# RWKV-7 chunk recurrence: two dependent products per chunk, or one prebuilt map

## The chip, the core and the metric

One Trainium2 chip, one of its cores, one launch. The metric is the device time of that core in microseconds (us), the median of repeated executions. The profile's own execution is told apart from them below.

## What is computed

A two-layer decoder step for 512 prompt positions and 8 x 4 sample positions, width 1024, 16 heads of 64. Layer A is RWKV-7 time mixing, layer B attention in three dilated windows. The part that matters here is layer A's scan over the prompt, for each head a 64 x 64 state:

```python
def wkv_step(state, inp):
    r, w, k, v, kk, b = inp
    sa = jnp.einsum('bhij,bhj->bhi', state, kk)
    state = state * w[:, :, None, :] - sa[..., None] * b[:, :, None, :] + v[..., None] * k[:, :, None, :]
    return state, jnp.einsum('bhij,bhj->bhi', state, r)

wkv, ys = lax.scan(wkv_step, wkv_prev.astype(f32), seq)
```

The outputs `ys` go through a group norm and a gate to the layer's output; the last state is an output too.

## The kernel before

All activations lie with features on the partitions: eight tiles of 128 features (two heads each), 544 positions (512 prompt, 32 sample). `dense` (L152) does the projections: each fp32 weight tile is split into a high and a low part, and three matmuls of 256 or 288 columns per 128 features of input give one output tile. Layer A needs 40 such projections, layer B 88.

The scan is done in 8 chunks of 64 positions. With the decays folded into the operands, a chunk is linear: its corrections solve a triangular system of 64 x 64, whose inverse T is computed once (`tinv`, `tmerge`), and then the new state and the outputs follow from the old state and the chunk's values. Head pairs p = 0 to 7 are processed one after the other and partly side by side. For each p:

- `pre_a`, `pre_b`, `gram` build the scaled operands: RH (receptance), BK (per chunk, 64 columns of b and 64 of k), AK (masked products with k, and the keys kk transposed). `tinv` runs on DVE for two head pairs at once, 62 dependent operations; `tmerge` joins its blocks on PE.
- `prechain(p)`, L607: T is multiplied into AK, 32 matmuls of 64 x 64 x 64, copied by ACT. The result WW is the left operand that turns [state; values] into the corrections u.
- `feed(p, i)`, for the chunks 2i and 2i+1, needs two PSUM buffers of tag "u" (there are two in all; `tmerge`, `prechain` and `gn` use them too). It forms Q = BK^T RH for both heads (L624, names qvp and qbp after their buffers) and masks it on DVE (L631), transposes the values (L628) and copies them on DVE to the lower half of `mv` (tiles of 128 rows: 64 of state, 64 of values), multiplies BK by the chunk's decay on POOL (L641), transposes it (L643), and copies it back on ACT.
- `step(p, i)` runs the two chunks one after the other. Per chunk and head: u = WW^T mv (L656); ACT copies u beside the values into `uv` (line of the helper `mv_`, L104; POOL has copied the values there); state product BK^T uv (L661); DVE adds the decayed old state and writes the next chunk's `mv` (L671); outputs from the state (L675) and from `uv` with Q (L678) into one sum. DVE copies the pair's outputs to Y.

Two chunks of one head pair depend on each other through L656, the ACT copy, L661 and L671. Different head pairs, feeds, and the projections of z and v are independent of that chain.

The order of the program is a list of tokens (`PLAN`: K, r, v, z are projections, a, b, e the operands, T, M, P the inverse, F a feed, C a step, G, I the group norm). The framework's scheduler turns it into one order for each engine when the kernel is built: it takes the tokens' order as priority, its own estimate of durations, and the free buffers. So each engine's order is fixed before the run, and an engine waits at its next instruction whatever stands behind. `NQ` = 4 fed chunk pairs may be ready at a time. `ENG` says which engine does a copy (s is ACT, v DVE, g POOL).

## Time and profile before

| what | us |
|---|---|
| median of 3 runs (1506.02 to 1510.37) | 1506.65 |
| the profiled execution | 1502.82 |
| its span, first to last instruction | 1501.0 |
| PE busy (matmuls; their pipelined ends are modelled) | 1373.4 |
| DVE busy | 989.5 |
| ACT busy | 654.1 |
| POOL busy | 531.5 |
| mean granted PE clock, 1 is full speed | 0.925 |

The profile gives each engine's instructions by line of the kernel. An fp32 matmul appears as two instructions. In a group's row stand the line, the engine, the operation, the tile that it writes and those that it reads, the shapes and the count; then the busy time and the mean of one in ns, and the idle time of that engine just ahead, with the engine and line that ended it. A timeline's row begins with the start and the duration in us. PE is the matmul, PEld the load of its weights.

### The profile page before, as it was taken

How to read it: one execution, taken by the hardware profiler on the slowest of the kernel's cores; microseconds unless marked ns; L12 is line 12 of the kernel's file. 1: busy time of each engine (PE TensorE's matmuls, PEld its weight loads, DVE VectorE, ACT ScalarE, POOL GpSimd, SP SyncE). 2: the span in 40 equal slices, each digit the busy share in tenths (PEclk: the TensorE clock that was granted, in tenths of full speed). 3: DMA queues.
4: the chain of work that ended last, by engine and by line, in shares of the span. 5: the costliest groups of instructions: out<-in, count | busy, mean ns of one | idle time of the engine just before them, and what ended most of it. 6: DMA issues, size and time to landing. Idle time of an engine off the chain costs nothing.

```text
span 1501.0 us, 32052 instructions
## 1 busy us (share of the span) xinstructions
PE 1373.4 (91%) x12144; PEld 1161.3 (77%) x12144; DVE 989.5 (66%) x2612; ACT 654.1 (44%) x1808; POOL 531.5 (35%) x763
## 2 busy tenths in 40 slices
PE   2999879998988998999889899999999999999986
PEld 2777868676767666989777779989799888998776
DVE  7428594747677546798996869756568554685434
ACT  5448353333342355444543435545355543644321
POOL 6124365434545221796867686000000000000121
PEclk9999978765879698999999999999999999999988
DMA  4123636224243113456344583445734356344632
GB/s 145 46 80 132 201 97 157 62 56 122 66 123 72 38 43 116 150 165 202 90 136 147 171 269 120 145 142 164 256 111 151 129 194 232 103 152 136 227 116 102
DMA packets 140587, 201.26 MB, mean 134 GB/s; under 512 B 76864, under 2 KB 80640, under 8 KB 140432
## 3 DMA queue, kind: packets, MB, share of 16 engines
q1 hardware_dynamic: 121456, 137.48, 29.9%
q10 hardware_dynamic: 16416, 54.41, 10.8%
q0 software_dynamic: 2560, 7.31, 1.4%
q8 instruction: 96, 1.57, 0.4%
q14 instruction: 59, 0.48, 0.1%
HBM read 150.90 MB, written 34.87 MB: 124 GB/s over the span
## 4 chain that ended last, share of the span: by engine, by line
PE 42%; DVE 8%; DMA 3%; ACT 1%; issue 1%; SPq 1%; ACTq 0%; DVEq 0%
PE dps L152 29%; DVE wlo L139 4%; PE sps L1014 3%; PE ptp L1075 2%; PE spo L1170 2%; PE ops L1091 1%; DMA swp<-nat 1%; PE ops L1087 1%; PE sc L1126 1%; SPq L945 1%; PE sc L1137 1%; PE sc L1132 1%; PE vtp L975 1%; DVE swp L947 1%; DMA vc<-in_vc 1%
## 5 line engine op out<-in xcount | busy, mean ns | idle before, releaser
L152 PE MATMUL dps<-hn,whi 128*128 128x256 f32 (+1 forms) x2560 | 509.3, 294 | 8.2 <-DVE vt L964 2.4
L152 PEld LDWEIGHTS dps<-hn,whi 128*128 128x128 f32 x2560 | 405.3, 189 | 31.0 <-issue 19.0
L152 PE MATMUL dps<-hn,wlo 128*128 128x288 f32 (+1 forms) x1280 | 373.6, 292 | 5.0 <-DVE wlo L139 4.6
L138 ACT ACTIVATE whi<-wst,prm 128x128 fp32r<-128x128 f32 x640 | 202.1, 391 | 223.2 <-PE dps L152 173.4
L139 DVE SCALAR_TENSOR_TENSOR wlo<-wst,prm,whi 128x128 fp32r<-128x128 f32 x640 | 252.7, 450 | 35.2 <-ACT whi L138 34.6
L152 PE MATMUL dps<-x,whi 128*128 128x256 f32 (+1 forms) x1024 | 229.7, 317 | 27.4 <-ACT x L166 11.0
L152 PEld LDWEIGHTS dps<-hn,wlo 128*128 128x128 f32 x1280 | 242.8, 190 | 12.7 <-DVE wlo L139 7.6
L152 PEld LDWEIGHTS dps<-x,whi 128*128 128x128 f32 x1024 | 178.1, 207 | 52.1 <-issue 15.9
L134 POOL TENSOR_TENSOR wlo<-wst,whi 128x1024 fp32r<-128x1024 f32 x48 | 118.5, 2469 | 191.9 <-ACT whi L133 179.3
L152 PE MATMUL dps<-x,wlo 128*128 128x288 f32 (+1 forms) x512 | 158.2, 310 | 0.0
L152 PEld LDWEIGHTS dps<-x,wlo 128*128 128x128 f32 x512 | 106.4, 208 | 2.6 <-issue 1.8
L1100 POOL COPY qd<-Q 64x32 f32<-64x32 f32 x48 | 12.7, 265 | 266.4 <-DVE Q L950 143.2
L1298 POOL TENSOR_TENSOR sS<-sS,sT 128x256 f32<-128x256 f32 x128 | 102.6, 802 | 8.3 <-DMA sS<-in_stN 0.2
L152 PE MATMUL dps<-g,whi 128*128 128x288 f32 (+1 forms) x512 | 102.2, 296 | 2.9 <-DVE ho L869 1.4
L133 ACT CAST whi<-wst 128x1024 fp32r<-128x1024 f32 x48 | 50.3, 1047 | 93.8 <-PE dps L152 61.3
L152 PEld LDWEIGHTS dps<-g,whi 128*128 128x128 f32 x512 | 82.1, 191 | 6.4 <-DVE g L167 2.9
L946 DVE TENSOR_TENSOR nat<-nat,cosn 128x544 f32<-128x544 f32 x48 | 36.5, 760 | 66.4 <-DMA swp<-nat 65.5
L152 PE MATMUL dps<-g,wlo 128*128 128x256 f32 (+1 forms) x256 | 74.1, 290 | 0.0
L1029 ACT ACTIVATE s<-s,nm 128x256 f32<-128x256 f32 (+1 forms) x128 | 61.7, 484 | 20.1 <-DVE nm L1026 20.0
L1107 POOL COPY pk<-vt 128x32 f32<-128x32 f32 x24 | 5.4, 225 | 161.1 <-DVE vt L964 108.6
L1014 PE MATMUL sps<-K,Q 64*128 64x128 f32 (+1 forms) x384 | 55.1, 321 | 6.4 <-DVE st L1020 4.0
L307 DVE SCALAR_TENSOR_TENSOR mix<-xn,prm,mix 128x512 f32<-128x512 f32 x48 | 42.4, 884 | 26.0 <-ACT mix L305 25.9
(315 smaller groups left out, 2433.6 us busy)
## 6 DMA issues: line engine op xcount, KB each, us to landing
wst<-in_wb SPq DMA_DIRECT2D x88, 512.0 KB
kc<-in_kc ACTq DMA_DIRECT2D x48, 512.0 KB
vc<-in_vc ACTq DMA_DIRECT2D x48, 512.0 KB
wst<-in_wa SPq DMA_DIRECT2D x40, 512.0 KB
swp<-nat SPq DMA_DIRECT2D x192, 68.0 KB
out_kT<-K SPq DMA_DIRECT2D x24, 272.0 KB
out_vT<-vt SPq DMA_DIRECT2D x24, 272.0 KB
xt<-in_xT SPq DMA_DIRECT2D x8, 272.0 KB
```

The lines of the kernel that those rows point to most:

```text
L133: nc.scalar.copy(hi, st)
L134: nc.gpsimd.tensor_tensor(lo, st, hi.bitcast(F32), op=ALU.subtract)
L138: nc.scalar.mul(hi[:, kt], st[:, kt], g)
L139: nc.vector.scalar_tensor_tensor(lo[:, kt], st[:, kt], g, hi[:, kt].bitcast(F32), op0=ALU.mult, op1=ALU.subtract)
L152: nc.tensor.matmul(ps[:, :n], lhsT=a[:, kt, :], rhs=x[:, c0:c0 + n], start=(kt == 0 and i == 0), stop=(kt == KT - 1 and i == 2))
L307: nc.vector.scalar_tensor_tensor(m[:, 0:NP_], xn[kt][:, 0:NP_], pv(s, kt), m[:, 0:NP_], op0=ALU.mult, op1=ALU.add)
L946: nc.vector.tensor_tensor(nat, nat, cosn, op=ALU.mult)
L1014: nc.tensor.matmul(ps[h][:, j, o], lhsT=Q[g][r, q], rhs=K[g][r, ks], start=True, stop=True)
L1029: nc.scalar.activation(s[:, b, lo:], s[:, b, lo:], AF.Exp, bias=nm[:, b:b + 1], accum_out=stats[:, b, h, 1:2])
L1075: nc.tensor.transpose(ps[:, b], st["s", l, h][:, b, half * P:(half + 1) * P], self.ident)
L1170: nc.tensor.matmul(po[32 * j:32 * j + 32, 0:256], lhsT=pT[:, i, 32 * j:32 * j + 32], rhs=vc[:, j], start=(i == 0), stop=False, skip_group_ ...
L1298: nc.gpsimd.tensor_tensor(s, s, t, op=ALU.add)
```

## The change

The chunk's map is built in the feed, ahead of the step. `prechain` makes the transposed WT (16 matmuls of 64 rows, 64 outputs and 128 columns in place of 32 of 64 columns, L608). `feed` writes the masked Q (L631) and the transposed BK (now three ACT copies, since each head's parts go to different places) into one tile `yz`, multiplies it by WT in PSUM (new, L650: 64 rows, 128 outputs, 128 columns, one per chunk and head, into the same two PSUM buffers), and adds what belongs to the values (DVE, L655) and to RH (DVE, L656 of the changed file); two ACT copies ("zz") bring over the state's map. So `yz` holds, for 128 rows of [state; values], 64 columns that give the outputs and 64 that give the next state. `step` is then per chunk and head one product for the state (L666), the same DVE update (L675), and one product for the outputs (L679). `uv` and its copies are gone. In `ENG`, the values' copies `mv` and the outputs' copy `ye` move from DVE to ACT. `PLAN`, the buffers and the rest stay.

```diff
-           w="ss", mv="vv", uv="gg", bt="s", kt="v", pr="s", ak="s", yc="s", ye="v", bo="gg", w1="ssss", tt="s")
+           w="ss", mv="ss", bt="s", kt="v", pr="s", ak="s", yc="s", ye="s", bo="gg", w1="ssss", tt="s")
...
             def prechain(p):
...
-                    for h in range(2):
-                        o = 128 * c2 + 64 * h
-                        for m in (0, 64):
-                            nc.tensor.matmul(ps[e][m:m + 64, o:o + 64], lhsT=ak[q, c2, h, m:m + 64],
-                                             rhs=t[q, 2 * c2 + h, :], start=True, stop=True)
+                    for h, r in enumerate(RH2):
+                        o = P * c2
+                        nc.tensor.matmul(ps[e][r, o:o + P], lhsT=t[q, 2 * c2 + h, :], rhs=ak[q, c2, h, :],
+                                         start=True, stop=True)
...
             def feed(p, i):
...
-                qq = QQ[p, i] = sp.tile([P, 2, 2, 64], F32, name="Q", tag="Q", bufs=NQ)
+                x = YZ[p, i] = sp.tile([P, 2, 2, P], F32, name="yz", tag="Q", bufs=NQ)
                 for h in range(2):
-                    nc.vector.tensor_tensor(qq[:, h], pq[h][:, 0:128].rearrange("p (e x) -> p e x", e=2),
+                    nc.vector.tensor_tensor(x[:, :, h, 0:64], pq[h][:, 0:128].rearrange("p (e x) -> p e x", e=2),
                                             msk[:, None, 1, :].to_broadcast([P, 2, 64]), op=ALU.mult)
...
-                self.mv_("bt", b2.rearrange("p c x -> p (c x)"), pq[1][:, 256:512])
+                b = pq[1][:, 256:512].rearrange("p (e h x) -> p e h x", e=2, h=2)
+                self.mv_("bt", x[:, :, 0, 64:128], b[:, :, 0, :])
+                self.mv_("bt", x[RA, :, 1, 64:128], b[RB, :, 1, :])
+                self.mv_("bt", x[RB, :, 1, 64:128], b[RA, :, 1, :])
+                for e in range(2):
+                    for h, r in enumerate(RH2):
+                        nc.tensor.matmul(pq[h][:, P * e:P * e + P], lhsT=w[r, e, i, :], rhs=x[r, e, h, :],
+                                         start=True, stop=True)
+                for h, r in enumerate(RH2):
+                    o = RH2[1 - h]
+                    v = pq[h][:, 0:256].rearrange("p (e x) -> p e x", e=2)
+                    nc.vector.tensor_tensor(x[o, :, h, :], v[o], x[o, :, h, :], op=ALU.add)
+                    nc.vector.tensor_tensor(x[r, :, h, 0:64], v[r, :, 0:64], rh[r, 2 * i:2 * i + 2, :], op=ALU.add)
+                    self.mv_("zz", x[r, :, h, 64:128], v[r, :, 64:128], h)
...
             def step(p, c2):
...
-                        nc.tensor.matmul(ps[r, o:o + 64], lhsT=WW[p][:, e, c2, h, :], rhs=mv[:, e, h, :],
+                        nc.tensor.matmul(ps[r, o:o + 64], lhsT=x[:, e, h, 64:128], rhs=mv[:, e, h, :],
                                          start=(e == 0), stop=True, skip_group_check=True)
-                    for h, r in ((0, RA), (1, RB)):
-                        self.mv_("ue", uv[RA, e, h, :], ps[r, o:o + 64], h)
-                    for h, r in ((0, RA), (1, RB)):
-                        nc.tensor.matmul(ps[r, o + 64:o + 128], lhsT=BK[p][:, c, 64 * h:64 * h + 64],
-                                         rhs=uv[:, e, h, :], start=False, stop=True,
-                                         skip_group_check=True)
...
-                    for h, r in ((0, RA), (1, RB)):
-                        nc.tensor.matmul(ps[r, y:y + 64], lhsT=mv[r, e, h, :], rhs=RH[p][r, c, :],
-                                         start=False, stop=False, skip_group_check=True)
-                    for h, r in ((0, RA), (1, RB)):
-                        nc.tensor.matmul(ps[r, y:y + 64], lhsT=uv[:, e, h, :], rhs=qq[:, h, e, :],
+                    for h, r in enumerate(RH2):
+                        nc.tensor.matmul(ps[r, y:y + 64], lhsT=mv[:, e, h, :], rhs=x[:, e, h, 0:64],
                                          start=False, stop=True, skip_group_check=True)
```

The built order moves with it on every engine. PE of before, at the third feed of head pair 5 (buffers qvp_5420, qbp_5421) and the steps beside it:

```order
L624 MATMUL qvp_5420<-rT_3111,bk_3235 64x64 x4
L628 MATMUL qvp_5420<-ident_58,vT_3349 64x128 x2
L643 MATMUL qbp_5370<-ident_58,bk_3235 128x128 x2
L675 MATMUL cps_5394<-rT_3111,mv_5354 64x64 x2
L678 MATMUL cps_5394<-Q_5351,uv_5391 64x64 x2
L656 MATMUL cps_5394<-mv_5354,ak_3241 64x64 x2
L747 MATMUL ysp_6041<-ident_58,yt_6039 128x32
L624 MATMUL qbp_5421<-rT_3111,bk_3235 64x64 x4
L661 MATMUL cps_5394<-uv_5391,bk_3235 64x64 x2
L656 MATMUL cps_5445<-mv_5384,ak_3241 64x64
L747 MATMUL ysp_6046<-ident_58,yt_6044 128x32
L675 MATMUL cps_5394<-rT_3111,mv_5354 64x64 x2
```

PE of the changed kernel at the same feed (buffers qvp_5278, qbp_5279; L650 is the new product, its first two rows here are the feed before):

```order
L650 MATMUL qvp_5230<-yz_5242,ak_3200 128x128 x2
L650 MATMUL qbp_5231<-yz_5242,ak_3200 128x128 x2
L624 MATMUL qvp_5278<-rT_3070,bk_3194 64x64 x4
L628 MATMUL qvp_5278<-ident_58,vT_3308 64x128 x2
L666 MATMUL cps_5312<-mv_5245,yz_5242 64x64
L624 MATMUL qbp_5279<-rT_3070,bk_3194 64x64 x4
L666 MATMUL cps_5312<-mv_5245,yz_5242 64x64
L643 MATMUL qbp_5279<-ident_58,bk_3194 128x128 x2
L679 MATMUL cps_5312<-yz_5242,mv_5245 64x64 x2
L666 MATMUL cps_5312<-mv_5245,yz_5242 64x64 x2
L650 MATMUL qvp_5278<-yz_5290,ak_3200 128x128 x2
L650 MATMUL qbp_5279<-yz_5290,ak_3200 128x128 x2
```

Before, the transposes L643 of a feed stand well behind its products L624, and the next feed's products ahead of them. Now one step matmul stands between the two, two step groups between L643 and L650, and one (L679) between L650 and the next feed.

ACT of the changed kernel for the same two feeds (Y is the outputs' copy, mv the values', yz the map's):

```order
L104 COPY mv_5245<-qvp_5230 64x2x64 x2
L104 COPY Y_4552<-cps_5264 128x128
L104 COPY yz_5242<-qbp_5231 128x2x64
L104 COPY yz_5242<-qbp_5231 64x2x64 x2
L104 COPY yz_5242<-qvp_5230 64x2x64
L104 COPY yz_5242<-qbp_5231 64x2x64
L104 COPY mv_5293<-qvp_5278 64x2x64 x2
```

and of before, where the copies of two head pairs' corrections stand between those of the feeds:

```order
L104 COPY uv_5391<-cps_5394 64x64 x2
L748 COPY YS_349<-ysp_6026 128x32
L104 COPY uv_5310<-cps_5313 64x64 x2
L104 COPY bk_3235<-qbp_5340 128x256
L748 COPY YS_349<-ysp_6031 128x32
L748 COPY YS_349<-ysp_6036 128x32
L104 COPY bk_3235<-qbp_5370 128x256
L104 COPY uv_5391<-cps_5394 64x64 x2
```

Five copies of a feed now follow one another on ACT, with the feed's values ahead of them. Between the stretch's last projection and the end of the recurrence, PE's order holds 5 feeds and 8 steps before, and 8 feeds and 11 steps now.

More of the change, by code (lines that the diff above doesn't have):

```diff
@@ L590, in tmerge @@
                     self.mv_("tt", t[q, :, 32:64], ps[q, 0:256].rearrange("p (c t) -> p c t", c=8))
-            TT, WW, Y = ([None] * 8 for _ in range(3))
-            QQ, MV = {}, {}
+            TT, WT, Y = ([None] * 8 for _ in range(3))
+            YZ, MV = {}, {}
+            RA, RB = slice(0, 64), slice(64, 128)
+            RH2 = (RA, RB)
             def prechain(p):
-                ak, bk, rh, t = AK[p], BK[p], RH[p], TT[p]
+                ak, t = AK[p], TT[p]
                 w = ak.rearrange("p c h x -> p (c h x)")
-                WW[p] = w.rearrange("p (e c h x) -> p e c h x", e=2, c=4, h=2)
+                WT[p] = w.rearrange("p (e c x) -> p e c x", e=2, c=4)
                 ps = [U8("wwp") for _ in range(2)]
@@ L611, in prechain @@
                 Y[p] = np_.tile([P, 560], F32, name="Y", tag="N")[:, 0:NT]
-            RA, RB = slice(0, 64), slice(64, 128)
             def feed(p, i):
-                bk, rh = BK[p], RH[p]
+                bk, rh, w = BK[p], RH[p], WT[p]
                 pq = [U8("qvp"), U8("qbp")]
@@ L620, in feed @@
                     c = 2 * i + e
-                    for h in range(2):
-                        r = slice(64 * h, 64 * h + 64)
+                    for h, r in enumerate(RH2):
                         for m in (0, 64):
-                            nc.tensor.matmul(pq[h][m:m + 64, 64 * e:64 * e + 64], lhsT=bk[r, c, m:m + 64],
+                            o = m if h == 0 else 64 - m
+                            nc.tensor.matmul(pq[h][o:o + 64, 64 * e:64 * e + 64], lhsT=bk[r, c, m:m + 64],
                                              rhs=rh[r, c, :], start=True, stop=True)
@@ L646, in step @@
+                for h, r in enumerate(RH2):
[4 more added lines that the diff above has]
+                    self.mv_("zz", x[r, :, h, 64:128], v[r, :, 64:128], h)
             def step(p, c2):
-                uv = sp.tile([P, 2, 2, 64], F32, name="uv", tag="uv", bufs=2)
@@ L649, in step @@
[L649 to L651 removed]
+                mv, x = MV[p, c2], YZ[p, c2]
                 ps = C8("cps")
                 for e in range(2):
[L654 to L656 removed]
+                    c, o = 2 * c2 + e, 64 * e
+                    for h, r in enumerate(RH2):
+                        nc.tensor.matmul(ps[r, o:o + 64], lhsT=x[:, e, h, 64:128], rhs=mv[:, e, h, :],
```

18 lines of the change are left out of this document (7 added, 11 removed).

## The prediction, made before the result was known

> **What bounds the kernel now.** I read the page first, for the busy shares, the granted clock and the chain that ended last.
>
> ```profile
> PE 1373.4 (91%) x12144; PEld 1161.3 (77%) x12144; DVE 989.5 (66%) x2612; ACT 654.1 (44%) x1808; POOL 531.5 (35%) x763
> ...
> PEclk9999978765879698999999999999999999999988
> ...
> PE 42%; DVE 8%; DMA 3%; ACT 1%; issue 1%; SPq 1%; ACTq 0%; DVEq 0%
> ```
>
> PE is busy nine tenths of the span, and what the chain names is mostly PE. The clock digits show one bad place: slices 6 to 14. Then I asked for the windows of the stretch in which the recurrence runs and of what follows.
>
> ```profile
> 255.00:575.00 320.00, 290.21 (x3501) 215.92 (x3501) 203.21 (x605) 126.00 (x349) 128.19 (x216) 0.76 0.28 75
> 575.00:1501.00 926.00, 875.66 (x7162) 775.96 (x7160) 632.82 (x1692) 400.23 (x1206) 290.77 (x410) 0.98 0.48 158
> ```
>
> The columns are the stretch, its length, then busy time of PE, PEld, DVE, ACT and POOL, the clock, DMA share and GB/s. The recurrence takes 320 us. PE is idle for 30 of them, and its mean clock is 0.76 against 0.98 afterwards. If the clock is either 1.0 or 0.5, as the short windows below suggest, then 48% of the stretch, 154 us, is at half. Everything after 575 us is projection work that the change does not touch, so a microsecond of PE time gained or lost in the stretch is one of the span.
>
> ```profile
> 430.00:450.00 20.00, 15.56 (x194) 11.14 (x194) 18.36 (x60) 6.46 (x19) 6.34 (x10) 0.50 0.11 35
> ...
> 500.00:522.00 22.00, 20.57 (x173) 13.99 (x173) 7.84 (x29) 5.77 (x26) 3.89 (x10) 0.53 0.09 30
> 522.00:527.00 5.00, 5.00 (x37) 4.23 (x37) 4.15 (x9) 3.78 (x5) 0.85 (x3) 0.66 0.03 7
> 535.00:565.00 30.00, 27.63 (x356) 15.54 (x356) 15.39 (x52) 17.08 (x44) 8.30 (x16) 1.00 0.21 66
> ```
>
> These show three regimes. At 430 DVE is the bound (the triangular inverse), and PE idles. At 500 PE runs the small recurrence matmuls nearly without a gap, yet at half clock; the projection that begins at 522 brings the clock back. At 535 the same small matmuls run at full clock. So PE is the bound for most of the stretch, and the next question is how much of its idle time is the chain of chunks. The waits of PE between 255 and 575 us (total, times, longest):
>
> ```profile
> PE cps L675 <- DVE mv L671: 8.4, 8, 2.3
> PE atp L524 <- DVE ak L517: 4.7, 1, 4.7
> PE cps L656 <- DVE mv L104: 3.3, 2, 3.1
> ...
> PE cps L661 <- ACT uv L104: 2.1, 4, 0.7
> PE cps L656 <- DVE mv L671: 1.4, 2, 1.0
> ```
>
> Only 8.4 + 2.1 + 1.4 = 11.9 us of PE's idle time is charged to the chain that the change shortens. The chain is long, but the order fills it with other heads' work.
>
> **PE's own work.** A pair of chunks (one feed and one step; there are 32) now has 8 groups of matmuls in the step, each of 4 instructions of 64 columns. After the change it has 4 in the step, and two new groups in the feed (after's L650) of 4 instructions each, 64 rows by 128 columns. The prechain's matmuls (L607) become half as many of twice the width: nothing. For the prices I take starts of consecutive groups in the timeline:
>
> ```profile
> 265.58 1.16 PE L411 MATMUL lps<-hid,lb 64*128 64x256 f32 x2
> 266.67 0.48 PE L675 MATMUL cps<-rT,mv 64*64 64x64 f32 x4
> ...
> 500.23 0.45 PE L624 MATMUL qbp<-rT,bk 64*64 64x64 f32 x8
> 500.61 0.34 PE L656 MATMUL cps<-mv,ak 128*64 128x64 f32 x4
> ...
> 500.84 0.61 POOL L641 TENSOR_TENSOR bk<-bk,plp 128x256 f32<-128x256 f32 x1 [0.49 <-PE qbp L624]
> ...
> 508.68 0.48 PE L675 MATMUL cps<-rT,mv 64*64 64x64 f32 x4
> 509.09 0.48 PE L678 MATMUL cps<-Q,uv 128*64 128x64 f32 x4
> ...
> 509.96 0.69 PE L624 MATMUL qbp<-rT,bk 64*64 64x64 f32 x8
> 510.58 0.48 PE L661 MATMUL cps<-uv,bk 128*64 128x64 f32 x4
> ...
> 526.56 0.33 PE L675 MATMUL cps<-rT,mv 64*64 64x64 f32 x4
> 526.82 0.34 PE L678 MATMUL cps<-Q,uv 128*64 128x64 f32 x4
> ...
> 540.77 0.44 PE L643 MATMUL qbp<-ident,bk 128*128 128x128 f32 x2
> 541.13 0.34 PE L656 MATMUL cps<-mv,ak 128*64 128x64 f32 x4
> 541.64 0.27 PE L624 MATMUL qbp<-rT,bk 64*64 64x64 f32 x2 [0.17 <-DVE mv L104]
> ...
> 541.87 0.28 PE L624 MATMUL qvp<-rT,bk 64*64 64x64 f32 x4
> 542.09 0.41 PE L628 MATMUL qvp<-ident,vT 128*64 128x128 f32 x2
> ```
>
> A step group costs 0.26 us at full clock (526.56 to 526.82) and 0.41 at half (508.68 to 509.09), so the four that go are worth 1.04 or 1.64 us a pair. No row shows the new matmul. Its nearest rows are two groups of 8 of 64 rows and 64 columns, the same number of columns in all: 2 x 0.38 = 0.76 us at full clock (500.23), 2 x 0.62 = 1.24 at half (509.96). The other is the only one with 64 rows and all 128 outputs: 2 instructions of 256 columns in 1.09 us at half (265.58 to 266.67), so 2.18 for the 1024 columns needed, and by the ratio 0.41/0.26 1.38 at full. I take the middle of the two, 1.07 and 1.71, since the new operation has the rows of the first and the outputs of the second. That is +0.03 or +0.07 us a pair: **+2 us** for 32. Ends: the second row throughout gives +0.34 and +0.54, +14 us; the interleaved row (16 instructions from 541.64 to 542.09, 0.45 us, and 0.71 at half) gives -0.59 and -0.93, -24 us. So fewer matmuls (512 instructions less of 12144), but no less PE time.
>
> That last end is where a rule of the Trainium skill speaks. The page "TensorE: Matmul & The Clock Gate", section "Part 3: Packing small matmuls", says that matmuls on different row groups run concurrently, and the two new groups do use different halves of the rows. The trace agrees where the halves alternate (541.64); in the changed order the four of one half stand ahead of the four of the other in most places. The sum by the rule is the second rival.
>
> **The chain.** A chunk's chain was matmul, two ACT copies, matmul, two DVE updates; it becomes matmul, two updates. The 2.1 us of waits on ACT go. Of the 9.8 us on the updates (8.4 + 1.4) I take 4, because the updates stay and the waits come mostly where DVE is full: **-6 us**, with -2 and -12 as ends. What is late next is the feed.
>
> **The feed.** Other work per pair, by these groups:
>
> ```profile
> L671 DVE SCALAR_TENSOR_TENSOR mv<-mv,plp,cps 64x64 f32<-64x64 f32 x112 | 31.2, 278 | 38.9 <-PE cps L661 29.0 <-PE cps L656 4.4 <-ACT bk L104 1.6
> ...
> L104 ACT COPY uv<-cps 64x64 f32<-64x64 f32 x128 | 26.4, 206 | 70.8 <-PE cps L656 62.2 <-DVE tX L548 5.4 <-DVE lam L723 2.3
> ...
> L104 POOL COPY uv<-mv 64x128 f32<-64x128 f32 x64 | 21.7, 339 | 53.8 <-DVE mv L104 19.2 <-PE cps L656 14.2 <-PE cps L678 9.3
> L641 POOL TENSOR_TENSOR bk<-bk,plp 128x256 f32<-128x256 f32 x32 | 20.5, 640 | 55.1 <-PE qbp L624 54.9
> ...
> L104 DVE COPY mv<-qvp 64x128 f32<-64x128 f32 x64 | 18.1, 283 | 1.4
> ...
> L104 ACT COPY bk<-qbp 128x256 f32<-128x256 f32 x32 | 11.9, 373 | 36.3 <-PE qbp L643 23.4 <-DVE mv L671 3.7 <-issue 2.7
> ...
> L631 DVE TENSOR_TENSOR Q<-qvp,msk 128x128 f32<-128x128 f32 x32 | 9.2, 287 | 5.5 <-PE qvp L628 5.1
> L104 DVE COPY Y<-cps 128x128 f32<-128x128 f32 x32 | 9.1, 288 | 15.7 <-PE cps L678 15.4
> ...
> L516 DVE TENSOR_TENSOR ab<-gps,msk 128x256 f32<-128x256 f32 x16 | 6.7, 418 | 10.5 <-PE gps L510 10.5
> ```
>
> ACT loses 4 x 0.206 + 0.373 = 1.20 us a pair and gets eight copies of 128 columns at an estimated 0.26 (on the line between 0.206 at 64 and 0.373 at 256): 2.1. Over 32 pairs that makes 126 busy us some 155 of 320, covered by PE. POOL loses its two copies (21.7 us in all), of no worth at 128 busy of 320, except that the multiply L641 no longer queues behind them. SP issues the same DMAs.
>
> DVE loses three copies, 0.85 us, and gets two adds at 0.418 (the 256-column row) and two at 0.287: 1.41. That is +0.56 a pair, 18 us in all. It counts where DVE is the bound, as at 430; elsewhere PE covers it. I take **+3 us**, between nothing and 18.
>
> The feed now holds both PSUM buffers of its tag through a longer chain: products (L624), POOL's multiply, transposes, three ACT copies, the new matmuls, DVE adds and ACT copies; only then can the next feed's products start. In the changed order nothing but one or two step matmuls stands between the products and the transposes in 14 of the 32 feeds (the order of before has a step's groups or the next feed there). The multiply ends 0.84 us after the products' last issue (500.84 + 0.61 against 500.61), and one step matmul covers 0.13 to 0.2 of it, so 0.65 to 0.7 is bare. The other links (one ACT copy 0.26 ahead of the first new group; adds of 0.418 + 0.287 ahead of the next products) are just covered by the two step groups and the second new group, with 0.1 left. So 0.8 us a bare feed, **+11 us**. Ends: half the feeds covered by luck, +5; every feed bare at 1.0, +32.
>
> **Sum.** 2 - 6 + 3 + 11 = +10 us. The profiled execution took 1502.8 us (span 1501.0), so 1512.8 by it; the median of the runs, 1506.65, is 3.8 above that execution, which makes 1517 as a median. A measurement of this kernel can tell about 0.3% from no change, 4.5 us, so this is slower.
>
> **Rivals.** *The chain's waits are what drops the clock* (the other side: faster). 154 us at half clock cost 154 x (1 - 0.26/0.41) = 56 us. If the waits at 255 to 575 are what lets the clock fall and their loss removes 40% of these phases, that is -22 us, and with the terms above -12: 1495; if the feed's waits are also covered, -23: 1484. It decides from some 28 us less at half on (28 x 0.37 = 10, and the sum is zero). For it: the two windows at half clock above both hold idle PE time. Against it: the feed's new waits sit in the same places. Chance 0.24.
>
> *The two halves of the new matmuls overlap*: -24 in place of +2 for PE, sum -16: 1491. Against it stands the printed order. Chance 0.10.
>
> *The waits fall in each other's shadow*: PE stays the bound, the feed's waits cost no more than the chain's did, 6, and the sum is +5 or less: 1507 to 1511. Chance 0.14.
>
> *The tail runs at half clock* (slower still). In the changed order the last projection of the stretch stands ahead of 8 feeds and 11 steps; before, of 5 and 8, and that tail ran at 1.00 (535 to 565). The feed and step matmuls of the tail are 8 x (0.38 x 2 + 0.36 x 2 + 1.07) + 11 x 4 x 0.26 = 32 us at full clock (0.36 from 540.77, also for L628), 50 at half: +18 over the forecast, 1535. For it: at 500 the clock fell with PE idle for no more than 1.4 of 22 us and stayed down until a projection. Chance 0.18. The Trainium skill, in the same page's "Part 1: The HAM clock gate", has the clock fall after about 3.4 us without work; by that rule waits of 0.8 us would never do it and this rival would be out. The window at 500 does not bear that out.
>
> **Chances.** The forecast, +5 to +16 us, has 0.34; with the tail rival that is 0.52 slower. The first two rivals give 0.34 faster, the shadow 0.14 same. The range reaches down to the first rival's full form, 1481, and up past the tail rival, 1540; about a tenth is left out on each side. The likeliest case by itself spans 1512 to 1523.
>
> **What would show it.** Right: in 255 to 575 PE's busy time hardly changes; waits of PE on ACT copies ahead of L661 are gone; new waits appear ahead of the transposes (on POOL) and of the next feed's products; the recurrence ends some 10 us later than now. Wrong: PE's time per new group near 0.25 us, or a mean clock well above 0.76 in the stretch; or no PE wait at the transposes.

## The result, and the profile after

| what | before | changed |
|---|---|---|
| median, us | 1506.34 | 1579.49 (1576.81 to 1586.73) |
| profiled execution, us | 1502.82 | 1578.39 |
| its span, us | 1501.0 | 1576.6 |
| mean granted PE clock | 0.925 | 0.891 |
| stretch of the recurrence, from 255 us to its last L678 / L679 | 319 | 385 |
| PE idle in it | 30 | 63 |
| time at half clock in it (twice what the mean clock lacks of 1, by its length) | 153 | 270 |

The ratio is 1.049, interval 1.045 to 1.053: slower by 73 us, where +10 was forecast. Clock, idle time and half-clock time are those of the one profiled execution, and the clock is given to two digits, so half-clock time is good to some 4 us. The page of the changed kernel, busy shares, clock by slices, and the chain by engine:

```profile
PE 1406.3 (89%) x11632; PEld 1186.2 (75%) x11632; DVE 1012.0 (64%) x2644; ACT 680.9 (43%) x1904; POOL 503.6 (32%) x699
...
PEclk9998977775666765899999999999999999999988
...
PE 59%; DVE 21%; DMA 7%; ACT 4%; issue 4%; POOL 3%; SPq 2%; DVEq 0%; ACTq 0%; POOLq 0%
```

The low digits of the clock now reach from the sixth slice to the sixteenth, and DVE's share of the chain that ended last went from 8% to 21%. Windows of the changed kernel (columns as in the prediction): the stretch, what follows it, and two pieces of the stretch's end.

```profile
255.00:640.00 385.00, 322.13 (x3017) 239.58 (x3017) 219.67 (x647) 152.52 (x444) 101.88 (x152) 0.65 0.23 62
640.00:1576.60 936.60, 877.25 (x7165) 777.60 (x7164) 639.04 (x1694) 401.41 (x1209) 292.30 (x410) 0.98 0.48 157
...
564.00:611.00 47.00, 40.65 (x377) 29.12 (x378) 17.55 (x58) 15.56 (x54) 3.35 (x7) 0.50 0.05 15
574.00:640.00 66.00, 55.51 (x452) 34.15 (x450) 25.43 (x79) 28.47 (x78) 3.96 (x8) 0.59 0.08 23
```

and the same cut of before, of which the prediction had shown the cut at 575:

```profile
255.00:574.00 319.00, 289.21 (x3499) 215.92 (x3501) 202.24 (x604) 125.40 (x349) 128.19 (x216) 0.76 0.28 75
574.00:1501.00 927.00, 876.66 (x7164) 775.96 (x7160) 633.78 (x1693) 400.82 (x1207) 290.77 (x410) 0.98 0.48 158
```

The span grew by 75.6 us: 66 in the stretch and 9.6 just behind it. The stretch's 66 are 33 of idle PE (385 - 322 against 319 - 289) and 33 of busy PE. Is the latter more work? With the price of the half clock from the prediction (a group takes 0.41 in place of 0.26, so 37% of the busy time at half clock would be saved) the busy time at full clock would be 289 x (1 - 0.37 x 0.48) = 238 us before and 322 x (1 - 0.37 x 0.70) = 239 now. So the work of PE is the same to what this working can tell (a step of 0.01 in the clock is 1 us here), and about 32 us are the clock. The waits of PE in the changed stretch (total, times, longest):

```profile
PE qvp L624 <- ACT yz L104: 9.3, 14, 1.6
PE qbp L643 <- POOL bk L641: 7.6, 6, 4.6
PE cps L679 <- DVE mv L675: 7.5, 9, 2.1
PE qbp L643 <- DVE yz L631: 5.5, 2, 4.6
...
PE qvp L650 <- ACT yz L104: 3.3, 8, 0.8
...
PE qbp L643 <- DVE tT L546: 2.3, 1, 2.3
PE qbp L643 <- DVE mv L675: 1.8, 5, 0.4
PE qbp L624 <- ACT yz L104: 1.6, 4, 0.6
```

Seven of these eight rows are waits of the feed's instructions: 31.4 us. Three single waits make up 11.5 of them:

```profile
293.27 0.66 PE L643 MATMUL qbp<-ident,bk 128*128 128x128 f32 x2 [2.35 <-DVE tT L546]
362.35 0.66 PE L643 MATMUL qbp<-ident,bk 128*128 128x128 f32 x2 [4.60 <-DVE yz L631]
478.89 0.69 PE L643 MATMUL qbp<-ident,bk 128*128 128x128 f32 x2 [4.57 <-POOL bk L641]
```

There the feed's own operation stood in an engine's order behind other work: ahead of the first two, DVE does steps of a triangular inverse (L546, L548) and operands before it comes to the mask L631; ahead of the third, POOL does three products of L717, 3.7 us, before the multiply L641. So some 20 us are waits at the links of the feed's chain itself. In before the feed's own waits were these:

```profile
PE qbp L624 <- DVE mv L104: 0.6, 2, 0.4
PE qbp L643 <- POOL uv L104: 0.5, 1, 0.5
PE qvp L624 <- DVE mv L104: 0.5, 1, 0.5
```

1.6 us, and 0.2 more on ACT's copy of BK. A feed in the tail shows what the waits alone don't (start, duration; 594.31 and 601.50 are the starts of two successive feeds):

```profile
594.31 0.69 PE L624 MATMUL qvp<-rT,bk 64*64 64x64 f32 x8 [0.70 <-ACT yz L104]
...
596.12 0.69 PE L624 MATMUL qbp<-rT,bk 64*64 64x64 f32 x8
...
596.90 0.61 POOL L641 TENSOR_TENSOR bk<-bk,plp 128x256 f32<-128x256 f32 x1 [6.16 <-PE qbp L624]
...
597.57 0.69 PE L643 MATMUL qbp<-ident,bk 128*128 128x128 f32 x2
...
598.30 0.82 ACT L104 COPY yz<-qbp 128x128 f32<-128x128 f32 x3 [1.84 <-PE qbp L643]
...
599.03 0.58 PE L650 MATMUL qvp<-yz,ak 64*128 64x128 f32 x1
...
599.97 0.42 PE L650 MATMUL qbp<-yz,ak 64*128 64x128 f32 x1
...
600.36 0.43 DVE L655 TENSOR_TENSOR yz<-qvp,yz 64x256 f32<-64x256 f32 x1 [0.83 <-PE qvp L650]
...
601.19 0.26 ACT L104 COPY yz<-qvp 64x128 f32<-64x128 f32 x1 [1.78 <-DVE yz L656]
...
601.50 0.69 PE L624 MATMUL qvp<-rT,bk 64*64 64x64 f32 x8 [0.70 <-ACT yz L104]
```

From the second row on, each waits for the one above: products, multiply, transposes, copies, map, adds, copy, next products, one engine after another (the second stands behind transposes and a step group in PE's order). That is 7.2 us for a feed. Of these PE is marked idle for little more than the 0.70 in brackets, because step groups stand between, at half clock (0.50 in the window from 564). So that the chain and not PE's own work at half clock sets this pace is a reading of the releasers, and no run shows it by itself. In before, at full clock (1.00 from 535 to 565), two feeds could follow each other in 2.2 us:

```profile
537.62 0.45 PE L624 MATMUL qvp<-rT,bk 64*64 64x64 f32 x8
...
539.78 0.45 PE L624 MATMUL qvp<-rT,bk 64*64 64x64 f32 x8
```

The last rows of the stretch's last projection, of before and of the changed kernel:

```profile
534.32 0.29 PE L152 MATMUL dps<-x,wlo 128*128 128x288 f32 x1
```

```profile
558.51 0.29 PE L152 MATMUL dps<-x,wlo 128*128 128x288 f32 x1
```

So the tail without projections took 39 us (to 574) and takes 81 (to 640), for 8 feeds in place of 5. Its mean clock was 0.95 and is 0.60: 4 us at half clock before, 65 now. With the same price, 0.37 x 0.80 x 67 us busy against 0.37 x 0.10 x 35, the tail's clock costs 19 us more than before. That is more than half of the 32; the other 13 or so lie ahead of the tail.

### The profile page after: what moved, and what is told of

Its sections match the earlier page's. It is cut to its first block, busy times and chain, and to the rows that moved or that the text cites. A ratio compares the mean times of both kernels' runs of the same rounds, so it can differ in the third digit from the quotient of the medians.

```text
span 1576.6 us, 31079 instructions
## 1 busy us (share of the span) xinstructions
PE 1406.3 (89%) x11632; PEld 1186.2 (75%) x11632; DVE 1012.0 (64%) x2644; ACT 680.9 (43%) x1904; POOL 503.6 (32%) x699
## 4 chain that ended last, share of the span: by engine, by line
PE 59%; DVE 21%; DMA 7%; ACT 4%; issue 4%; POOL 3%; SPq 2%; DVEq 0%; ACTq 0%; POOLq 0%
PE dps L152 35%; DVE wlo L139 4%; DVE tX L548 3%; PE sps L1015 2%; DVE tT L546 2%; PE ptp L1076 2%; PE spo L1171 1%; PE qvp L650 1%; PE cps L666 1%; PE ops L1092 1%; PE hps L378 1%; DVE mix L307 1%; DMA swp<-nat 1%; PE ops L1088 1%; DMA vc<-in_vc 1%
## 5 line engine op out<-in xcount | busy, mean ns | idle before, releaser
L152 PE MATMUL dps<-hn,whi 128*128 128x256 f32 (+1 forms) x2560 | 510.1, 294 | 7.9 <-DVE vt L965 2.4
L152 PEld LDWEIGHTS dps<-hn,whi 128*128 128x128 f32 x2560 | 406.4, 190 | 30.1 <-issue 18.8
L152 PE MATMUL dps<-hn,wlo 128*128 128x288 f32 (+1 forms) x1280 | 374.1, 292 | 5.6 <-DVE wlo L139 5.4
L152 PE MATMUL dps<-x,whi 128*128 128x256 f32 (+1 forms) x1024 | 230.2, 317 | 33.1 <-ACT x L166 11.3
L152 PEld LDWEIGHTS dps<-hn,wlo 128*128 128x128 f32 x1280 | 243.5, 190 | 13.1 <-DVE wlo L139 8.1
L152 PEld LDWEIGHTS dps<-x,whi 128*128 128x128 f32 x1024 | 179.1, 208 | 58.3 <-issue 16.1
L152 PE MATMUL dps<-x,wlo 128*128 128x288 f32 (+1 forms) x512 | 157.5, 309 | 0.0
L152 PEld LDWEIGHTS dps<-x,wlo 128*128 128x128 f32 x512 | 106.7, 209 | 2.4 <-issue 1.8
L152 PE MATMUL dps<-g,whi 128*128 128x288 f32 (+1 forms) x512 | 101.9, 295 | 3.6 <-DVE ho L870 1.4
L152 PEld LDWEIGHTS dps<-g,whi 128*128 128x128 f32 x512 | 81.9, 191 | 7.0 <-DVE g L167 2.8
L152 PE MATMUL dps<-g,wlo 128*128 128x256 f32 (+1 forms) x256 | 74.0, 289 | 0.0
L641 POOL TENSOR_TENSOR bk<-bk,plp 128x256 f32<-128x256 f32 x32 | 19.7, 615 | 126.2 <-PE qbp L624 126.2
```

The source lines that it names most:

```text
L152: nc.tensor.matmul(ps[:, :n], lhsT=a[:, kt, :], rhs=x[:, c0:c0 + n], start=(kt == 0 and i == 0), stop=(kt == KT - 1 and i == 2))
```

## The experiments

Theory F: the feed holds its two u buffers through a longer chain, feeds follow one another at that chain's pace, and the waits also keep the clock down (the expectations call a rival S as well: the step's new form or the map's own matmuls). Rivals: E, the copies moved to ACT; T, the tail without projections; O, the order: before had a lucky or tuned one, and any other costs tens of us. In the table the stretch is from 255 us to the last output product, and its idle and half-clock time come from its window as above, of the one profiled execution. The stretches of e7 and e10 hold some 150 and 100 of PE's instructions more, projections that stand behind the stretch in the kernel that they were made from.

| run | median, us | ratio to before | stretch | idle | at half clock |
|---|---|---|---|---|---|
| e1_before_eng | 1523.8 | 1.016 | 339 | 43 | 170 |
| e2_after_dve | 1583.4 | 1.056 | 397 | 71 | 286 |
| e3_after_u3 | 1546.3 | 1.030 | 359 | 54 | 208 |
| e4_after_ownbk | 1577.8 | 1.051 | 385 | 59 | 270 |
| e5_before_hold | 1572.9 | 1.048 | 377 | 50 | 264 |
| e6_after_split | 1551.2 | 1.033 | 355 | 55 | 213 |
| e7_before_u3 | 1574.9 | 1.048 | 401 | 55 | 257 |
| e8_after_fill | 1625.7 | 1.078 | 433 | 39 | 303 |
| e9_before_null | 1532.9 | 1.017 | 349 | 32 | 216 |
| e10_after_z3 | 1587.0 | 1.053 | 401 | 62 | 281 |
| e11_before_hold_half | 1556.8 | 1.032 | 359 | 51 | 215 |
| e12_after_burst | 1588.7 | 1.053 | 399 | 60 | 263 |
| e13_after_split_u3 | 1543.4 | 1.020 | 361 | 52 | 224 |
| e14_after_null | 1576.8 | 1.045 | 387 | 52 | 294 |
| e15_before_split | 1542.1 | 1.021 | 357 | 50 | 214 |
| e16_before_null2 | 1517.6 | 1.008 | 319 | 36 | 128 |
| e17_before_null3 | 1534.4 | 1.021 | 343 | 28 | 206 |
| e18_before_split_null | 1550.8 | 1.032 | 373 | 58 | 239 |

The ratios carry intervals of 0.4 to 1.1 per cent to either side, 6 to 17 us. Single executions of before beside these runs went from 1486 to 1514 us, at mean clocks between 0.913 and 0.933, and their medians from 1504 to 1509. Each loss below is against the median of before beside it; each gain is against the 1579.5 of the changed kernel.

**Were it the copies on ACT?** On before alone, `mv="vv"` to `mv="ss"` and `ye="v"` to `ye="s"`:

> The kernel before, with only the engine table of the change: the copies of the values (mv) and of the outputs (ye) on ACT in place of DVE. Theory F (the feed's longer chain holds its two PSUM buffers, PE waits bare at its links, and the waits also let the clock fall): this edit has no part in it, within 6 us of 1506, mean clock 0.92 or 0.93. Rival E (the copies on ACT make up the feed's delay, since they queue there): at least 20 us of the 73 show already here, 1526 or more.

On the changed kernel, the reverse:

> The changed kernel, with mv and ye back on DVE. Theory F: the chain that holds the buffers (products, decay, transposes, copies, map, adds) is unchanged, so 0 to 10 us back: 1569 to 1580. Rival E: 20 us or more back, 1560 or less.

+17 on before, which is outside F's bound and just under E's; its interval, +11 to +38 us, reaches past E's, so this run alone does not decide. On the changed kernel nothing is given back (+4, where F had 0 to 10 back and E 20 or more). The +17 is not more than what a swap of tokens costs (below). E falls by the second run.

**A longer hold, on before, without any work of PE.**

```diff
                 self.mv_("bt", b2.rearrange("p c x -> p (c x)"), pq[1][:, 256:512])
+                hold = sp.tile([P, 256], F32, name="hold", tag="hold", bufs=1)
+                for j in range(3):
+                    nc.scalar.copy(hold, pq[1][:, 256:512])
+                nc.scalar.copy(hold[:, 0:128], pq[0][:, 0:128])
```

> The kernel before, whose feed holds its two PSUM buffers longer for nothing: after the transposes' copy, four more ACT copies (some 1.3 us) read the buffers into a tile that nobody uses. PE's work is unchanged. Theory F (what costs is the buffers' hold, by waits of PE in order and by the clock that falls after them): 20 to 60 us slower, with new waits of PE ahead of L624 on ACT's copy, and more of the stretch at half clock. Rival S (the step's new form or the map's own matmuls cost the time): within 8 us of 1506, since ACT has room (126 of 320 us busy).

and with one copy of each in place of three and one:

> The kernel before, whose feed holds its buffers for two ACT copies more (some 0.65 us) in place of four (1.3 us, which cost 66 us). Theory F: less than with four, 15 to 45 us slower than before. Rival O (any other order costs about the same, whatever the hold): 55 us or more, or no trend at all.

The stretch of before with the long hold:

```profile
255.00:632.00 377.00, 327.12 (x3502) 239.54 (x3503) 202.85 (x612) 165.54 (x479) 126.82 (x216) 0.65 0.24 63
```

+66 and +48 us with the arithmetic of before untouched, ACT busy for less than half the stretch, and PE's work at full clock the same (242 and 240 by the working above, the short hold's clock being 0.70). The long hold makes a loss like the change's, in stretch, half-clock time and clock, with less idle time (50 against 63). One sign of F did not come: the new waits do not stand at L624 (1.0 us on the hold's copy) but at the steps, whose operands come later. In the profiled execution, 65 us longer than that of before, 20 are idle time in the stretch, 38 the clock, and 7 lie behind the stretch. And a longer hold also makes the scheduler draw a new order; what that alone can do comes below.

**A looser or shorter hold, on the changed kernel.** A third u buffer, for which one step buffer goes (`NPU = 3`, `NPC = 1`):

> The changed kernel with three PSUM buffers of tag u in place of two, and one of tag c in place of two (there are eight banks in all). A feed can begin its first products while the one before still holds its last buffer; steps of two head pairs can no longer overlap. Theory F: the waits of PE ahead of the products (9.3 us on yz) shrink below 4 us and 15 us or more of the 73 come back, less what the single step buffer costs. Rival T (the order itself: projections placed early, a tail of feeds and steps with nothing dense in it runs at half clock, whatever the waits): at most 10 us back, and the stretch after the last projection still at 0.6.

The feed rearranged, so that the u buffers are taken late:

```diff
+                b2 = sp.tile([P, 2, P], F32, name="bd", tag="bd", bufs=2)
+                nc.gpsimd.tensor_tensor(b2, bk[:, 2 * i:2 * i + 2], ...)
+                pt8 = T8("qtp")
...
+                    nc.tensor.transpose(pt8[:, 256 + P * e:384 + P * e], b2[:, e], self.ident)
...
+                pq = [U8("qvp"), U8("qbp")]
```

> The changed kernel with the feed rearranged: decay into a tile of its own, both transposes in one PSUM buffer of tag t, their copies first; the two buffers of tag u are taken only then, for products, mask, map and adds. So of the chain that holds the u buffers POOL's multiply, the transposes and the five copies are gone. Theory F: more than with a third buffer (which gave 33 us): 40 us or more back, 1540 or less, idle time of PE in the stretch near 35. Rival T (the order and its tail): 10 us or less back.

Both together:

> The changed kernel with the rearranged feed (decay and transposes ahead, out of the u buffers) and three u buffers, one step buffer: both edits that each gave back some 30 us. Theory F: together more than each, 1520 to 1540, what is left being the order's part. Rival O (the order's luck, not the hold): no better than one alone, 1545 or more.

And only the decayed BK in a tile of its own:

> The changed kernel with the decayed BK written to a tile of its own (two buffers), so that POOL's multiply no longer has to wait for the products L624 which read BK: one bare link of the feed goes. Theory F: waits of PE ahead of the transposes on POOL (7.6 us) go to under 2, and since fewer waits also leave the clock up, 20 to 40 us come back: 1540 to 1560. Rival T: 10 us or less back.

33, 28 and 36 us come back, and only 9, 8 and 11 of them are idle time in the stretch; half-clock time falls by 62, 57 and 46. F had expected at least 15 for the third buffer, which came, 40 or more for the rearranged feed, and 1520 to 1540 for both (1543 came). Its sign failed for the third buffer: the waits ahead of the products were to shrink from 9.3 us below 4, but they moved to the second buffer's products and grew from 10.9 us on both to 21.0 (5.9 of them one wait):

```profile
PE qbp L624 <- ACT yz L104: 20.7, 14, 5.9
```

With the rearranged feed they are 8.2 us and the idle time is 55, not near 35; with both edits 3.0. So the time that comes back does not follow these waits. Where the clock came back differs too. With the rearranged feed, alone and with the third buffer, the scheduler put projections later: the last one ends at 586 and 593 us, 24 and 23 us before the end of the recurrence, and the tail has 17 and 11 us at half clock in place of 65, which is most of what the first gained of it and all of what the second did. With the third buffer alone the tail is 73 us long with 54 at half clock, and the gain lies ahead of it (155 in place of 207). The two edits do not add up, and 36 to 45 us of the 73 stay. Taking one link out (e4) gave nothing, where F had expected 20 to 40 us; that is inside rival T's bound. Its longest wait shows where the time went:

```profile
PE qvp L624 <- ACT yz L104: 15.4, 16, 6.8
```

Waits on POOL no longer stand among the long ones, and those at the link where the buffer is given back grew from 9.3 to 15.4 (6.8 of them one wait). The link's wait moved and did not go.

The third buffer on before is the control:

> The kernel before with three buffers of tag u and one of tag c, the edit that gave the changed kernel 33 us back. Theory F: the feed of before is not bound by the u buffers, so nothing to gain, and one step buffer costs: 1506 to 1525. If the gain is general and not of the change's feed: 1490 or less.

+68, where F had at most 19: on before, three buffers for the feeds and one for the steps cost far more than I thought, and its waits are now those of the steps:

```profile
PE cps L675 <- DVE mv L671: 14.8, 12, 4.2
...
PE cps L656 <- DVE Y L104: 8.3, 15, 1.3
```

These are the update, which cost 8.4 us in before, and the copy of Y out of the one step buffer. So with these buffers the changed kernel is the faster of the two, by 29 us (1546.3 against 1574.9). In these two runs the sign of the change hangs on how the PSUM buffers are laid out.

**What does an order cost by itself?** Tokens of `PLAN` swapped on before, with all work, chains and buffers as they were: `C12 C7 b4` to `C7 C12 b4`; `v6 a7` to `a7 v6`; both of these and two more.

> The kernel before with two tokens of PLAN swapped (C7 ahead of C12), which changes nothing of the work and none of its chains, but moves about a tenth of PE's rows. Theory F (the feed's hold of its two buffers is what costs): 1490 to 1520, since no hold is longer. Rival O (PLAN was tuned for the one order that before has, and any other order loses tens of us): 1535 or more.

> The kernel before with another token of PLAN moved (a7 ahead of v6), again without change to work or chains; some 700 lines of PE's order differ. It gives a second value for what an order alone costs. Theory F: 1505 to 1535, as the first swap (1533) or less. Rival O: a wide spread, 1545 or more possible.

> The kernel before with four tokens of PLAN moved at once (the two swaps of 26 and 11 us and two more), work and chains unchanged; nearly a quarter of PE's rows move. If the level of 1542 to 1551 is what a new order costs: 1530 to 1555. If orders cost no more than the single swaps showed: 1510 to 1530, and the rest of the loss is the feed's.

One swap on the changed kernel:

> The changed kernel with one token of PLAN moved (a4 ahead of b5), which leaves all work and chains as they are and moves about a twentieth of PE's rows. Theory F: within 15 us of 1579, since the hold is the same. Rival O: the order's spread is as large as the loss, so 30 us or more away from 1579, to either side.

The rearranged feed on before, and one swap on that:

> The kernel before with the feed rearranged: decay into a tile of its own, both transposes in one buffer of tag t, ahead; the two u buffers hold only the products until they are masked. The hold is shorter than in before by the multiply, the transposes and their copy. Theory F with the order's part (some 20 us for any new order): 1500 to 1525, no more than the swap of tokens costs and possibly less than before. Rival O: like other changed orders without regard to the hold, 1530 or more.

> The kernel before with the rearranged feed (1542) and one token of PLAN moved (a7 ahead of v6). If its level is only the order's luck: 20 us or more away from 1542, most likely down. If it is a cost of the rearranged feed: within 10 us of 1542.

The stretch of before with the first swap:

```profile
255.00:604.00 349.00, 316.93 (x3501) 232.39 (x3501) 203.23 (x614) 127.76 (x350) 127.87 (x216) 0.69 0.27 70
```

Swaps alone cost before 24, 10 and 30 us against the runs of before beside them. The profiled execution of the middle one took 1505.8 us and shows no loss to explain; in the other two the idle time is unchanged (32 and 28 us), so the loss is clock. The order of before keeps 166 us of its stretch at full clock (319 - 153); the first swap keeps 133, the four 137. On the changed kernel the one swap tried costs nothing (-3; half-clock time 294 in its profiled execution). And the rearranged feed, whose hold is shorter, costs before 35 us, and with a token moved 46, where F had expected 1500 to 1525; F alone does not explain that. It gives a comparison under one feed, though: the changed arithmetic stands at 1551.2 there and the old one at 1542.1 and, with the token moved, 1550.8. That is 9 us or nothing, no more than these medians can tell. So the same change of arithmetic is worth +73 us in the layout of before, about 0 to 9 with the rearranged feed, and -29 with three u buffers.

The swaps move less of the order than the edits of the hold do. In the traces, the share of PE's instructions up to the end of the recurrence that stand in runs common with the kernel they came from is about 0.75, 0.81 and 0.63 for the three swaps on before, but 0.60 and 0.53 for the two holds, and 0.50 for the rearranged feed. On the changed kernel it is 0.88 for the swap and 0.72 to 0.97 for e2, e4, e10 and e12, all of which stay within 10 us of 1579, but 0.54, 0.54 and 0.38 for the three edits that give time back. So the edits of the hold are also those with the most new order, and these runs do not part the two. Against the order alone stand e5 and e17: with nearly the same share kept, the hold costs 66 us and the four tokens 30.

**Do waits lower the clock, and what raises it?** Two unwanted matmuls per feed, in the places where PE waits, then eight in a row in four feeds of the tail (no result of theirs is read):

```diff
+                nc.tensor.matmul(pq[0][64:128, 256:512], lhsT=self.ident[:, 0:64], rhs=vT[p][:, 0:256], start=True, stop=True)
```

> The changed kernel with two matmuls more per feed that compute nothing wanted (128 rows, 64 outputs, 256 columns, into a corner of the feed's buffer that is never read), one ahead of the transposes L643 and one between the two groups L650: 64 in all, some 0.35 us each at full clock, 22 us of PE time, in places where PE mostly waits. If waits of PE are what lets the clock fall (theory F's second half): the stretch's half-clock time falls by 40 us or more from 270, and the time is 1550 to 1575 in spite of more work. If the clock follows what kind of matmul runs (only projections bring it back): half-clock time unchanged or longer, 1585 to 1610.

> The changed kernel with a block of eight unwanted matmuls (128 rows, 64 outputs, 256 columns; by the kernel with 64 of them some 0.75 us each at full clock) in four feeds of the tail, ahead of L643: 32 in all, some 24 us of PE time at full clock, in four unbroken blocks of 6 us. If an unbroken block of work is what brings the clock back (as the projections seem to): the clock is 1.0 by the end of each block and for some us behind it, and the half-clock time of the stretch is 15 us or more below 270 in spite of the longer stretch; time 1578 to 1595. If only projections do it: blocks at half clock to their end, 1605 or more.

With the two in every feed the idle time fell to 39 us, and the time at half clock rose to 303:

```profile
255.00:688.00 433.00, 393.68 (x3147) 271.51 (x3147) 215.04 (x643) 153.37 (x445) 103.86 (x152) 0.65 0.21 55
```

So filling 24 of the 63 us of waits does not bring the clock back; F had expected 40 us less at half clock and 1550 to 1575. Their own work is more than I had estimated; the answer for their line gives the shortest, the median and the longest of the 128 instructions in ns:

```profile
L640 PE MATMUL qvp<-vT,ident x128: 379/634/690, 261.0 to 675.1; 128*64 128x256 f32 x128
```

At 379 ns, two for a matmul, they are 49 us at full clock, of which 24 went into former waits. With eight in a row from 573.2 us on it does come back, though of the 15 us less at half clock in the whole stretch that were expected there are 7. Windows of 2 us, PE busy and the clock near the end of the row:

```profile
576.00:578.00 2.00, 2.00 (x6) 1.04 (x5) 0.00 (x0) 0.00 (x0) 0.00 (x0) 0.50 0.00 0
578.00:580.00 2.00, 2.00 (x17) 1.06 (x15) 0.00 (x0) 0.32 (x2) 0.00 (x0) 0.97 0.00 0
580.00:582.00 2.00, 1.57 (x15) 1.27 (x16) 1.74 (x6) 0.84 (x4) 0.00 (x0) 1.00 0.00 0
582.00:584.00 2.00, 1.62 (x22) 1.08 (x22) 1.00 (x5) 0.82 (x4) 0.55 (x1) 1.00 0.00 0
584.00:586.00 2.00, 1.88 (x16) 1.60 (x17) 0.81 (x3) 0.78 (x3) 0.07 (x1) 0.74 0.00 0
```

Five microseconds of this block raise the clock; then PE waits 0.4 and 0.5 us, and the clock is down again some 6 us after the block's end (0.50 from 585 on). The next block raised it after 4.1 us (597.90 to 602), and then waits of 0.35 and 0.70 us did not bring it down. So it is not the length of a wait that decides, and no bound for it can be read here. Nor is a wait needed. The first two rows below are of the changed kernel, where PE is busy in every window from 330 to 350 and the clock still falls at 338; the third is of before, one of 26 windows from 297 to 323 that all read busy 1.00 and clock 0.50:

```profile
337.00:338.00 1.00, 1.00 (x15) 0.80 (x15) 0.65 (x3) 0.96 (x4) 0.29 (x1) 1.00 0.80 143
338.00:339.00 1.00, 1.00 (x5) 0.51 (x5) 0.62 (x4) 0.61 (x3) 0.47 (x2) 0.61 0.66 109
310.00:311.00 1.00, 1.00 (x13) 0.76 (x12) 0.54 (x2) 0.09 (x1) 0.00 (x0) 0.50 0.55 104
```

(The ends of matmuls are modelled, so short gaps inside a group would not show.) Unbroken small matmuls can thus stay at half clock for 26 us; what raised it there was a projection, after 4.0 us (319.98 to 324). So waits are not the whole cause of the low clock. That fits the swaps, which lost clock without more idle time, and it means that F's second half, that the waits keep the clock down, is not shown.

**The tail.** A third buffer for projections that wait for their norm (`NZ = 3`):

> The changed kernel with three buffers in place of two for the projections z that wait for their norm (tag Z), so that one projection more can run before the recurrence ends; in the built order it stands among the last steps. The 7.5 us that PE waits at the end for zg should go, and the clock should rise in the last steps. Theory T (a bare tail without projections is a large part): 12 to 25 us back, 1555 to 1567. Theory F alone: only that wait, 5 to 9 us back, 1570 to 1575.

The wait for zg behind the recurrence in the changed kernel, and the waits for zg with the third buffer:

```profile
651.96 0.80 PE L152 MATMUL dps<-x,whi 128*128 128x256 f32 x2 [7.45 <-DVE zg L808]
```

```profile
PE dps L152 <- DVE zg L808: 2.6, 2, 1.9
```

That wait went, the time at half clock did not (281 against 270), and the whole is 7 us slower, not 12 to 25 faster as T has it, nor 5 to 9 as F has it. Part of why: PE's waits come back some 20 us further on, 7.2 and 4.1 us ahead of L152 on ACT's copy of g (at 683.7 and 695.6), where the changed kernel has none. But it is no test of T. The projections that moved stand from 633.1 to 656 us, the last 23 us of the stretch, where the clock is 0.91; ahead of them, from 561 to 633, the tail is as bare as before, and its clock is 0.58. The runs with the rearranged feed, in which projections stand later, bear T out better: their tails have little time at half clock. In the runs made from before, the bare tails of e5 and e11 are 78 and 70 us long with 58 and 45 us at half clock, those of e9 and e17 59 and 55 us with 35 and 29, and that of before 39 with 4. So the tail's clock goes with the loss, whatever made the order, and a projection put into the middle of the tail of the changed kernel was not tried.

## Why the prediction was wrong, point by point

Of the span's 75.6 us, 33 are idle time in the stretch, 32 the clock there, 1 PE's work, and 9.6 lie behind the stretch. The forecast had +5 for the first (-6 and +11), nothing for the second and the last, and +2 for the work (and +3 for DVE). Two steps failed. The clock of the stretch was taken as it was, a term of nothing in the sum, though the tail at half clock had been priced as a rival; and the feed's waits were sized from what is bare at one link.

- **PE's streams, +2.** Right: 238 and 239 us at full clock.
- **The chain's waits, -6.** Near: the waits on the ACT copy ahead of L661 are gone (2.1), those on the two updates went from 9.8 to 7.5.
- **The feed's waits, +11, ends +5 and +32.** Right in kind and place (ahead of the transposes, the map and the next products), too small in size: 31.4 against 1.8 before, so +30, near the upper end. Some 18 of that are at the links of the chain; the step that failed there is "one step matmul covers 0.13 to 0.2 of it, so 0.65 to 0.7 is bare": I added up what is bare at each link and took the rest as covered, but the links are in series, through four engines, and where feeds follow one another they take 7.2 us. The other 11.5 are the three waits in which DVE's mask or POOL's multiply stood behind other work; the sum had no term for that.
- **The clock.** In the sum nothing; 18 us in a rival, for the tail alone, at a chance of 0.18. Measured some 32 us (half-clock time 153 to 270), 19 of them in the tail and the rest ahead of it. This is the larger miss. The forecast kept the tail at before's full clock (0.95 in its 39 us); it ran at 0.60. e9 and e17 show half-clock time move by 63 and 53 us with no more idle time than before, so a new order can do it, and in before's own rows PE stayed at half clock for 26 us without a gap. What did it in the changed kernel, the new order or the feed's waits, stays open.
- **DVE, +3.** Not separable. DVE's busy time in the stretch rose by 17 us (202 to 220), as the upper end had it, and two of the three long waits above are for DVE.
- **Behind the stretch, nothing.** Measured +9.6, of which 7.5 is PE waiting for a buffer of zg while the last norm is worked out; no term for it.
- **The rivals.** That fewer waits leave the clock up (1495) was the wrong way round. The tail at half clock, +18 at a chance of 0.18, came: 65 of its 81 us, +19. It was the rival that the sum should have had; alone it makes 1535, and the idle time makes the rest. The first rival's full form is 1484 by the sum; the range's end of 1481 has no working. The two halves of the map do overlap where their groups alternate: eight instructions from 599.03 to 600.32, where the next begins, 1.29 us at half clock against the 1.71 of the sum, but that changes nothing where the chain sets the pace.

So of the 73 us, where they lie is measured: idle time in the stretch, the tail's clock, the clock ahead of it, and 9.6 behind. What caused them is shown in part. Three edits that loosen or shorten the feed's hold give back some 30, no milder edit of the changed kernel does, and a hold added to before costs 48 and 66, more than any swap. That makes the hold a likely cause. It is not shown alone, since each of these edits also draws a new order, the gain is mostly clock, the waits it was to remove did not shrink in e3, the gain of e6 and e13 lies in a tail that projections fill, and a shorter hold did not help before (e15). A new order of before's own work, with nothing else changed, costs up to 30, all of it clock; that the changed kernel pays this too is likely from e15 and e18, which reach the level of e3, e6 and e13 with the old arithmetic. But it is argued: no kernel here has the new arithmetic in an order as good as before's. How the 73 us divide between hold and order stays open. None of these versions beats before.

## What to carry to other kernels

When work is moved out of a serial chain into a stage that runs ahead, write down the ahead stage's own chain, buffer to buffer, and multiply it by the number of times that it follows itself: compare that with the time PE gives it; a sum of the bare links alone was too small here. When a scheduler makes the order, any edit draws a new one, so measure a swap or two that change nothing before reading a few per cent as the edit's worth. Where the granted clock moves between half and full, count half-clock time as its own term of the sum: here it grew with idle time in some runs and without it in others. And look at what follows the last projection: more than half of the clock's loss lay in the tail behind it, where the forecast had the clock of the kernel before.

## What the runs showed of the hardware

The clock was the surprise. It also fell without a wait (338 us, above). Two rows of the changed kernel, with the idle time ahead of them in brackets, and the windows in which they lie:

```profile
561.55 0.34 PE L679 MATMUL cps<-yz,mv 128*64 128x64 f32 x4 [0.69 <-DVE mv L675]
562.70 0.34 PE L679 MATMUL cps<-yz,mv 128*64 128x64 f32 x4 [0.70 <-DVE mv L675]
```

```profile
558.00:562.00 4.00, 3.01 (x37) 2.03 (x35) 2.21 (x8) 1.98 (x5) 2.10 (x1) 1.00 0.00 0
562.00:564.00 2.00, 0.95 (x7) 0.65 (x8) 0.56 (x2) 0.79 (x3) 0.81 (x2) 0.88 0.35 94
564.00:566.00 2.00, 1.52 (x8) 1.23 (x8) 0.91 (x3) 0.34 (x2) 0.00 (x0) 0.50 0.43 168
```

Full speed becomes half within 3 us of two waits of 0.7 us, and stays there for 47 us; in e12 it fell after waits of 0.4 and 0.5 us. The blocks that raised it there took 4.9 and 4.1 us. The Trainium skill's page "TensorE: Matmul & The Clock Gate", section "Part 1: The HAM clock gate", has it rise after some 3.4 us of sustained work, with which the blocks agree within some 1.5 us, and fall after an idle window of 3.4 us, with which these rows do not: no wait there is half as long. The same page's section "A second HAM failure mode: psum-queue depth-cycling" says that short idles between groups of matmuls while PSUM buffers are cycled make the clock swing between half and full; the swing is what this kernel shows, though not what causes it, and for the size of it the runs give the number: the very same work of PE took 289 busy us in the order of before and 317 in that of e9, with idle times of 30 and 32 us.
